# Order of work on ScalarE and VectorE in a hybrid decoder layer: late weight splits, scalings, keys and norm sums

## The chip, the cores and the metric

The kernel runs on one core of one Trainium2 chip. A core has five engines with instruction queues of their own: TensorE (PE in the profile; PEld is its weight load), VectorE (DVE), ScalarE (ACT), GpSimd (POOL) and SyncE (SP), which here only issues DMAs. The metric is the device time of one execution in microseconds (us). The kernel before has a median of 1187.84 us over three runs, from 1185.57 to 1188.33.

## The reference

One decoder layer for 512 tokens of width 1024, in float32. The normalised input goes through one combined projection that feeds two mixers. Both are merged by sigmoid gates, projected, normalised and added to the stream; a gated MLP with a short causal convolution follows.

```python
h = rms_norm(x, norm_mix_pre); z = h @ w_in
z_rwkv, z_nsa, z_gate = split(z)
o_a = rwkv7_time_mix(z_rwkv, ...)   # 16 heads of 64: state recurrence over time,
                                    # then group norm of y, bonus (r*k*r_k summed)*v, times g = sigmoid(gd) @ g2
o_b = nsa_attention(z_nsa, ...)     # compressed, selected and window branches
g_a, g_b = split(sigmoid(z_gate))
m = g_a * (o_a @ w_branch_rwkv) + g_b * (o_b @ w_branch_nsa)
x = x + rms_norm(m @ w_out, norm_mix_post)
h = rms_norm(x, norm_ffn_pre)
u = causal_dwconv(h @ ffn_up)
u_gate, u_val = split(u)
x = x + rms_norm((silu(u_gate) * u_val) @ ffn_down, norm_ffn_post)
```

## The kernel before

**Number format.** A matrix product is made of three matmuls: both operands are split into a high part (rounded by ScalarE, tile names in h) and a low part (the remainder, names in l), and high x high, high x low and low x high are summed. A weight therefore passes through `split_to` (L156): a DMA on SP's queue into a raw buffer, a copy on ScalarE (L124 in the trace), a subtraction on GpSimd or VectorE (L160). The raw buffers are a ring of WB = 3 (tag "raw"): a fourth load waits until the subtraction of the first has read its buffer. SP's queue issues in order, so what stands behind a waiting load waits too.

**Stages.** The recurrence has eight pairs of heads, p = 0 to 7, in two groups of GP = 4 pairs, g = 0 and 1. For each pair `prep` (from L506) makes decay, keys and bonus factor F, then `couple` (from L573) makes the products g<-AR,KB within chunks of 64 tokens (L597), masks them into GS (L600), transposes the scaled keys into BKT (L620), and computes LV (L626) and the bonus bv (L631). `invert` inverts the small triangular blocks of all pairs of a group on VectorE (XP, L652 and L654, the copy at L666). `recur` walks through eight chunks: xw and xs are products with the inverse (L796), UV is their copy (L800 on VectorE, L801 on ScalarE), and xs with BKT (L806) carries the state. `finish` (from L821) scales the group's output YT by the group norm's factor (L831), transposes it (gt), adds the bonus, and multiplies by pg, the product of gate activations with the weights g2 (L861 to L864). While the second group is inverted and recurred, TensorE projects gates, v, the keys of the selected and window branches (ksp and kwp; `khl`, split into kst at L950 and L951) and the queries q. Then follow eight stages of attention scores and values, the branch projections (`branch`, ub, L1181 to L1183), the output projection (wo), the second norm with its transposes (n2p), and the MLP (pu, dn).

**What sets the order.** `drive` (L439) takes steps alternately from a chain of projections (the fill) and from streams that run beside it, each at its own rate, so the program text is written in an interleaved order. A scheduler then orders the instructions of each engine; it may move an instruction ahead of its place in the program. One that is marked `tc.keep_in_program_order` keeps its place in program order. PSUM banks come in named pairs (pj, px, py, pz); a name's third use waits for the readers of its first.

**Names the prediction uses.** g20r to g27r are the raw g2 weights and gh, gl their halves; lw5r and lw6r, with lh and ll, the small weights for decay and rate of pairs 5 and 6; pw, pa, pn and pb the four PSUM tiles in `prep` (decay, rate, norm sums, broadcast norm); T the decay after tanh; rbh and rbl the halves of F.

Of the kernel before, what the change touches and what calls it, by code (L numbers as in the profile page):

```python
# [12 lines left out]
AF = mybir.ActivationFunctionType  # L13
# [19 lines left out]
GP = 4  # L33
# [9 lines left out]
def hybrid_layer(ctx: ExitStack, tc: tile.TileContext, a, out, dbg=None, stop=None):  # L43
# [109 lines left out]
    eps6 = vec[:, V_EPS:V_EPS + 1]  # L153
    epsg = vec[:, V_EPS + 1:V_EPS + 2]

    def split_to(src, hi, lo, name, n, eng=None, p=None):  # L156
        raw = (p or wp).tile([128, n], F32, tag="raw", name=name + "r", bufs=WB)
        sy.dma_start(raw, src)
        act(hi, raw, AF.Copy)
        (eng or po).tensor_tensor(lo, raw, hi.bitcast(F32), op=OP.subtract)  # L160

    def split_w(src, name):
# [346 lines left out]
    def prep(p, o, gr=None):  # L509
# [17 lines left out]
        F = rw.tile([128, S], F32, tag="T", name=f"F{p}", bufs=NT)  # L527
        sc.activation(F, pa, AF.Identity, scale=hka[:, p:p + 1], bias=oka[:, p:p + 1])
        yield
        pn = pz(f"pn{p}")  # L530
        for t in range(4):
            te.matmul(pn[:, 2 * t:2 * t + 2], Q[:, t * 128:(t + 1) * 128], sel, start=True, stop=True)
        nt = rw.tile([128, 8], F32, tag="nt", name=f"nt{p}", bufs=2)
# [27 lines left out]
        ve.tensor_tensor(KB[:, :, 0, :], pb.rearrange(c8, t=64), A.rearrange(c8, t=64), op=OP.mult)  # L561
        o.Q = None if gr else Q
        ve.scalar_tensor_tensor(gr.AR[p % GP][:, 0, :] if gr else Q, Q, -2.0, pb, op0=OP.mult, op1=OP.mult)
        ve.scalar_tensor_tensor(F, R, vec[:, V_RK + p:V_RK + p + 1], F, op0=OP.mult, op1=OP.mult)
        rbh = o.rbh = rw.tile([128, S], F32R, tag="T", name=f"rbh{p}", bufs=NT)
        sc.activation(rbh, F, AF.Copy)
        rbl = o.rbl = rw.tile([128, S], F32R, tag="T", name=f"rbl{p}", bufs=NT)
# [253 lines left out]
    def finish(gr, g):  # L821
        st = gr.st
        yield
        ve.tensor_reduce(st[:, 1, 3], gr.sq[3], axis=AX.X, op=OP.add)
        sc.activation(st[:, 0], st[:, 1], AF.Sqrt, scale=1.0 / 64, bias=epsg)
        ve.reciprocal(st[:, 1], st[:, 0])
        yield
        for i in range(GP):
            p = GP * g + i
            Y8 = gr.YT[:, :, i]  # L830
            scaled = (po if g else ve).tensor_tensor(Y8, Y8, st[:, 1, :, 2 * i:2 * i + 2, None]  # L831
                                                     .to_broadcast([128, 4, 2, 64]), op=OP.mult)
            if g == 0:
                tc.keep_in_program_order(scaled)
            gh = rh_.tile([128, 256], F32R, tag="gh", name=f"gh{p}", bufs=1)
            gl = rh_.tile([128, 256], F32R, tag="gl", name=f"gl{p}", bufs=1)
            split_to(a["g2"][p], gh, gl, f"g2{p}", 256)
            po.tensor_copy(gh[64:96, 128:], gl[64:96, 128:].bitcast(F32))
            bvl = rh_.tile([128, S], F32, tag="bvl", name=f"bvl{p}", bufs=1)
            sy.dma_start(bvl, bvd[p])  # L840
            yield
            yield
            yield
            pt = px(f"gt{p}")
            for t in range(4):
                tr(pt[:, t * 128:(t + 1) * 128], Y8[:, t].rearrange("p h v -> p (h v)"), ident)
            y2 = rh_.tile([128, S], F32, tag="TB", name=f"y2{p}", bufs=1)
            y2v = y2.rearrange("p (t s u) -> p t s u", s=2, u=64)
            ptv = pt.rearrange("p (t s u) -> p t s u", s=2, u=64)
            lnw, lnb = vec[:, V_LNW + p:V_LNW + p + 1], vec[:, V_LNB + p:V_LNB + p + 1]  # L850
            if i % 2 == 0:
                sc.activation(y2, pt, AF.Identity, scale=lnw, bias=lnb)
            else:
                for x in range(2):
                    sc.activation(y2v[:, :, x], ptv[:, :, 1 - x], AF.Identity, scale=lnw, bias=lnb)
            (ve if g else po).tensor_tensor(y2, y2, bvl, op=OP.add)
            yield
            if g:
                yield
            pg = px(f"pg{p}")  # L860
            te.matmul(pg, gh[:, :128], lg1h, start=True, stop=False)  # L861
            te.matmul(pg, gh[:, :128], lg1l, start=False, stop=False)
            te.matmul(pg, gl[:, :128], lg1h, start=False, stop=False)
            te.matmul(pg, gh[:96, 128:], lg2, start=False, stop=True)  # L864
            ve.tensor_tensor(y2, y2, pg, op=OP.mult)
            sy.dma_start(oad[p], y2)
            yield
# [97 lines left out]
    def qproj(p8):  # L965
        return split_out(27 + p8, f"q{p8}", qd[p8], 0.125)

    fr1 = [plain_out(43 + i, f"v{i}", vd_[i], zp) for i in range(1, 4)]
    fr1 += [khl(39 + i, "ssww"[i], 0, False) for i in (0, 2)]
    drive(itertools.chain(*gates_(16 - 6 - NG0, zp), *fr1, *[qproj(i) for i in range(2)], *[x for i in range(2, NQ1)  # L970
                                        for x in ((qproj(i), queries(i - 2)) if i < 4 else (qproj(i),))]),
          f0, *rt1)
    rax.close()
# [198 lines left out]
    def branch(x, o8, sh, sl):  # L1172
# [1 line left out]
        sy.dma_start(g, gtd[o8, x])  # L1174
        wh, wl = split_w(a["wb"][x, o8], f"wb{x}{o8}")
        wh, wl = wslice(wh), wslice(wl)
        if x + o8 == 0:
            yield
        p = pj(f"ub{x}{o8}")
        for k in range(KT):  # L1180
# [82 lines left out]
    with pool("bp", "left") as bp:  # L1263
# [3 lines left out]
        for _ in fill:  # L1267
            next(load, None)
        run(load)
        for o8 in range(8):  # L1270
            run(branch(1, o8, spb[0], spb[1]))
            for i in (2 * o8, 2 * o8 + 1):
                if i < NW:
                    wo_load(i, bp)
# [122 lines left out]
    for t in range(4):  # L1397
        wo_tok(t, (px, py, pj, px)[t])
        if t < NU:
            first(t)  # L1400
        if t:
            norm_t(xn[t - 1], t - 1, h2h, h2l, "n2")
        xn[t] = norm_x(x2[:, t, :], t, [g2b[:, 0:512], g2b[:, 512:]], "n2", op)
    pu4 = [py("pu0"), py("pu1"), pj("pu2")]
    for b in range(NU - 1):
        half_up(b, 0)
    norm_t(xn[3], 3, h2h, h2l, "n2")
    half_up(NU - 1, 0)
# [151 lines left out]
```

## Time and profile before

| what | value |
|---|---|
| median of three runs | 1187.84 us (1185.57 to 1188.33) |
| the profiled execution's own time | 1192.53 us |
| its span, first to last instruction | 1190.7 us |
| mean granted TensorE clock | 0.988 |
| busy: TensorE, VectorE, ScalarE, GpSimd | 1158.1, 583.6, 582.3, 583.2 us |
| instructions: TensorE, VectorE, ScalarE, GpSimd | 7414, 1208, 1149, 525 |
| HBM read and written | 108.30 and 19.14 MB |

In the profile a row of the timeline has the start in us, the duration in us, engine, line, operation, out<-in, shape and count, and in brackets how long the engine had been idle before it and what ended that. A row of the waits has the waiting engine and line, what it waited for, the sum of its waits in us, their number and the longest. Lines are those of the kernel before.

### The profile page before, as it was taken

How to read it: one execution, taken by the hardware profiler on the slowest of the kernel's cores; microseconds unless marked ns; L12 is line 12 of the kernel's file. 1: busy time of each engine (PE TensorE's matmuls, PEld its weight loads, DVE VectorE, ACT ScalarE, POOL GpSimd, SP SyncE). 2: the span in 40 equal slices, each digit the busy share in tenths (PEclk: the TensorE clock that was granted, in tenths of full speed). 3: DMA queues.
4: the chain of work that ended last, by engine and by line, in shares of the span. 5: the costliest groups of instructions: out<-in, count | busy, mean ns of one | idle time of the engine just before them, and what ended most of it. 6: DMA issues, size and time to landing. Idle time of an engine off the chain costs nothing.

```text
span 1190.7 us, 19894 instructions
## 1 busy us (share of the span) xinstructions
PE 1158.1 (97%) x7414; PEld 927.2 (78%) x7414; DVE 583.6 (49%) x1208; ACT 582.3 (49%) x1149; POOL 583.2 (49%) x525
## 2 busy tenths in 40 slices
PE   7999999999999999999999999999999999999997
PEld 6888878876778777766767777788888888888886
DVE  4225655633556561488797775654333433331103
ACT  5536653543655434277776555443444444443311
POOL 4336664434566443366567653521456655654440
PEclk8999999998999999999999999999999999999999
DMA  6522235321342654234442225551133233334421
GB/s 221 132 81 74 87 102 164 107 81 46 87 140 82 179 156 155 65 114 135 132 143 78 65 72 187 183 182 45 53 97 98 97 98 98 98 96 134 132 63 71
DMA packets 95652, 131.95 MB, mean 111 GB/s; under 512 B 34178, under 2 KB 37058, under 8 KB 95299
## 3 DMA queue, kind: packets, MB, share of 16 engines
q1 hardware_dynamic: 79634, 116.26, 31.4%
q10 hardware_dynamic: 15920, 14.42, 3.9%
q8 instruction: 58, 0.95, 0.3%
q14 instruction: 40, 0.32, 0.1%
HBM read 108.30 MB, written 19.14 MB: 107 GB/s over the span
## 4 chain that ended last, share of the span: by engine, by line
PE 60%; DVE 5%; issue 3%; ACT 2%; POOL 2%; DMA 0%; DVEq 0%; ACTq 0%; POOLq 0%
PE pu L221 6%; PE pu L219 6%; PE pu L220 6%; PE o L1124 3%; PE dn L1293 3%; PE dn L1292 3%; PE dn L1291 3%; PE pt L140 3%; PE ub L1181 2%; PE s L1068 2%; PE ub L1183 2%; PE ub L1182 2%; PE q L297 1%; PE wo L1363 1%; PE wo L1365 1%
## 5 line engine op out<-in xcount | busy, mean ns | idle before, releaser
L1077 ACT ACTIVATE p<-p,stt 128x384 f32<-128x384 f32 (+3 forms) x128 | 70.8, 554 | 41.5 <-DVE stt L1075 39.8
L1431 DVE SCALAR_TENSOR_TENSOR u<-pu,cvec,u 128x511 f32<-128x511 f32 x44 | 33.0, 749 | 102.0 <-ACT u L1430 102.0
L1051 POOL TENSOR_SCALAR p<-p,stt 128x512 f32<-128x512 f32 (+3 forms) x60 | 68.6, 1153 | 27.7 <-DVE stt L1046 21.3
L1075 DVE CUSTOM_DVE_ANT_0 p<-s,rh 128x384 f32<-128x384 f32 (+3 forms) x128 | 59.4, 484 | 26.5 <-PE s L1061 19.0
L1435 POOL TENSOR_TENSOR u<-u,u 128x512 f32<-128x512 f32 x22 | 28.4, 1290 | 38.6 <-DVE u L1432 37.7
L1437 DVE TENSOR_TENSOR al<-u,ah 128x512 fp32r<-128x512 f32 x22 | 23.9, 1085 | 45.8 <-ACT ah L1436 45.8
L140 PE MATMUL pt<-ident,p 128*128 128x128 f32 x320 | 44.8, 273 | 0.8 <-POOL p L1051 0.7
L1124 PE MATMUL o<-PT,vt 128*64 128x256 f32 (+3 forms) x256 | 45.3, 444 | 0.0
L140 PEld LDWEIGHTS pt<-ident,p 128*128 128x128 f32 x320 | 37.9, 141 | 5.7 <-POOL p L1051 1.0
L1068 PE MATMUL s<-kst,qs 128*128 128x512 f32 (+1 forms) x128 | 38.5, 392 | 3.5 <-DVE stt L1075 3.5
L1430 ACT ACTIVATE u<-pu,cvec 128x512 f32<-128x512 f32 x44 | 33.6, 764 | 5.7 <-PE pu L1395 5.7
L1051 DVE TENSOR_SCALAR p<-p,stt 128x512 f32<-128x512 f32 (+3 forms) x68 | 34.0, 531 | 0.6
L1432 DVE SCALAR_TENSOR_TENSOR u<-pu,cvec,u 128x510 f32<-128x510 f32 x44 | 32.9, 749 | 1.6
L1124 PEld LDWEIGHTS o<-PT,vt 128*64 128x64 f32 x256 | 17.5, 136 | 18.8 <-issue 16.7
L1068 PEld LDWEIGHTS s<-kst,qs 128*128 128x128 f32 x128 | 21.2, 188 | 13.0 <-DVE stt L1075 8.4
L1115 ACT ACTIVATE PT<-pt 128x512 f32<-128x512 f32 x48 | 27.3, 584 | 5.4 <-PE pt L140 5.3
L1339 DVE TENSOR_TENSOR p2tm<-dn,gb 128x512 f32<-128x512 f32 x4 | 2.8, 692 | 51.2 <-ACT p2jl L1337 51.2
L1117 DVE COPY PT<-pt 128x512 f32<-128x512 f32 x32 | 21.8, 682 | 8.4 <-PE pt L140 8.3
L1436 ACT ACTIVATE ah<-u 128x512 fp32r<-128x512 f32 x22 | 13.9, 633 | 22.4 <-POOL u L1435 22.4
L1077 ACT ACTIVATION_READ_ACCUMULATOR p<-p,stt 128x1 f32 x128 | 24.1, 188 | 0.0
L801 ACT ACTIVATE UV<-xs 64x256 f32<-64x256 f32 x16 | 6.0, 378 | 34.7 <-PE xs L796 34.1
L654 DVE TENSOR_TENSOR XP<-XP,TM 128x30 f32<-128x30 f32 (+14 forms) x60 | 20.3, 338 | 2.0
(1758 smaller groups left out, 3960.4 us busy)
## 6 DMA issues: line engine op xcount, KB each, us to landing
gtd<-gt ACTq DMA_DIRECT2D x16, 256.0 KB, 2.2
qs<-qd SPq DMA_DIRECT2D x32, 128.0 KB, 2.9
g<-gtd SPq DMA_DIRECT2D x16, 256.0 KB, 3.1
xt<-in_x_dram SPq DMA_DIRECT2D x4, 512.0 KB, 5.7
bvd<-bv SPq DMA_DIRECT2D x8, 256.0 KB, 2.4
bvl<-bvd SPq DMA_DIRECT2D x8, 256.0 KB, 2.7
oad<-y SPq DMA_DIRECT2D x8, 256.0 KB, 2.9
kst<-kst ACTq DMA_DIRECT2D x16, 128.0 KB, 2.8
```

The lines of the kernel that those rows point to most:

```text
L140: return te.transpose(o, i, ident)
L219: te.matmul(p, wh(k), mh(k), start=first and k == 0, stop=False)
L220: te.matmul(p, wh(k), ml(k), start=False, stop=False)
L221: te.matmul(p, wl(k), mh(k), start=False, stop=last and k == n - 1)
L1051: (po if b and (p8 or e) else ve).tensor_scalar(o.pe[e, b, k], o.pe[e, b, k], st[e][:, 3, i:i + 1], None, op0=OP.mult)
L1068: m = te.matmul(s_[:, :n], qt, kt[:, x, b, :n], start=x == 0, stop=x == 1)
L1075: ve.tensor_tensor_reduce(sb, parts[b], rh[e][:, (3 - qb) * 128:], -1.0, BIG, OP.add, OP.min, st[e][:, 0, i:i + 1])
L1077: sc.activation(sb, sb, AF.Exp, scale=-1.0, bias=st[e][:, 0, i:i + 1], accum_out=st[e][:, 1, i:i + 1])
L1124: te.matmul(acc[e * 64:e * 64 + 64, j * 128:], vt[:, j, b * 256 + g * 64:b * 256 + g * 64 + 64], m[e][:, c:c + n], start=False, stop=k == ...
L1291: te.matmul(acc[half, t], sh[:, k, tsl], wh[kk], start=k == 0, stop=False)
L1292: te.matmul(acc[half, t], sh[:, k, tsl], wl[kk], start=False, stop=False)
L1293: te.matmul(acc[half, t], sl[:, k, tsl], wh[kk], start=False, stop=k == n - 1)
```

## The change

Seven edits, none of which alters a value that is computed.

A. `split_to` takes `late`; the copies of the g2 weights in `finish` are marked to keep their place on ScalarE.
B. The norm sums pn take a bank of the pair px instead of pz, except in pair 4.
C. YT's scalings in `finish` are issued two pairs ahead; in group 0 the first two may be moved freely, the third and fourth keep their place.
D. Beside the second group, the keys ksp and kwp and the query q0 are projected ahead of v1 to v3, and not behind them.
E. The bonus factor's multiplication F<-R keeps its place behind AR.
F. The first half of block 0 of the up projection is issued ahead of the transposes of the second norm's third row block.
G. In the second branch's projections, a branch issues its weight loads when the branch before is halfway.

```diff
--- before.py
+++ after.py
@@ -153,10 +153,12 @@
     eps6 = vec[:, V_EPS:V_EPS + 1]
     epsg = vec[:, V_EPS + 1:V_EPS + 2]
 
-    def split_to(src, hi, lo, name, n, eng=None, p=None):
+    def split_to(src, hi, lo, name, n, eng=None, p=None, late=False):
         raw = (p or wp).tile([128, n], F32, tag="raw", name=name + "r", bufs=WB)
         sy.dma_start(raw, src)
-        act(hi, raw, AF.Copy)
+        i = act(hi, raw, AF.Copy)
+        if late:
+            tc.keep_in_program_order(i)
         (eng or po).tensor_tensor(lo, raw, hi.bitcast(F32), op=OP.subtract)
 
     def split_w(src, name):
@@ -527,7 +529,7 @@
         F = rw.tile([128, S], F32, tag="T", name=f"F{p}", bufs=NT)
         sc.activation(F, pa, AF.Identity, scale=hka[:, p:p + 1], bias=oka[:, p:p + 1])
         yield
-        pn = pz(f"pn{p}")
+        pn = (pz if p == GP else px)(f"pn{p}")
         for t in range(4):
             te.matmul(pn[:, 2 * t:2 * t + 2], Q[:, t * 128:(t + 1) * 128], sel, start=True, stop=True)
         nt = rw.tile([128, 8], F32, tag="nt", name=f"nt{p}", bufs=2)
@@ -561,7 +563,8 @@
         ve.tensor_tensor(KB[:, :, 0, :], pb.rearrange(c8, t=64), A.rearrange(c8, t=64), op=OP.mult)
         o.Q = None if gr else Q
         ve.scalar_tensor_tensor(gr.AR[p % GP][:, 0, :] if gr else Q, Q, -2.0, pb, op0=OP.mult, op1=OP.mult)
-        ve.scalar_tensor_tensor(F, R, vec[:, V_RK + p:V_RK + p + 1], F, op0=OP.mult, op1=OP.mult)
+        tc.keep_in_program_order(ve.scalar_tensor_tensor(F, R, vec[:, V_RK + p:V_RK + p + 1], F, op0=OP.mult,
+                                                         op1=OP.mult))
         rbh = o.rbh = rw.tile([128, S], F32R, tag="T", name=f"rbh{p}", bufs=NT)
         sc.activation(rbh, F, AF.Copy)
         rbl = o.rbl = rw.tile([128, S], F32R, tag="T", name=f"rbl{p}", bufs=NT)
@@ -825,16 +828,23 @@
         sc.activation(st[:, 0], st[:, 1], AF.Sqrt, scale=1.0 / 64, bias=epsg)
         ve.reciprocal(st[:, 1], st[:, 0])
         yield
+        def scaled(i):
+            Y8 = gr.YT[:, :, i]
+            m = (po if g else ve).tensor_tensor(Y8, Y8, st[:, 1, :, 2 * i:2 * i + 2, None]
+                                                .to_broadcast([128, 4, 2, 64]), op=OP.mult)
+            if g == 0 and i > 1:
+                tc.keep_in_program_order(m)
+            return Y8
+
+        ahead = [scaled(i) for i in range(2)]
         for i in range(GP):
             p = GP * g + i
-            Y8 = gr.YT[:, :, i]
-            scaled = (po if g else ve).tensor_tensor(Y8, Y8, st[:, 1, :, 2 * i:2 * i + 2, None]
-                                                     .to_broadcast([128, 4, 2, 64]), op=OP.mult)
-            if g == 0:
-                tc.keep_in_program_order(scaled)
+            Y8 = ahead[i]
+            if i + 2 < GP:
+                ahead.append(scaled(i + 2))
             gh = rh_.tile([128, 256], F32R, tag="gh", name=f"gh{p}", bufs=1)
             gl = rh_.tile([128, 256], F32R, tag="gl", name=f"gl{p}", bufs=1)
-            split_to(a["g2"][p], gh, gl, f"g2{p}", 256)
+            split_to(a["g2"][p], gh, gl, f"g2{p}", 256, late=True)
             po.tensor_copy(gh[64:96, 128:], gl[64:96, 128:].bitcast(F32))
             bvl = rh_.tile([128, S], F32, tag="bvl", name=f"bvl{p}", bufs=1)
             sy.dma_start(bvl, bvd[p])
@@ -965,9 +975,9 @@
     def qproj(p8):
         return split_out(27 + p8, f"q{p8}", qd[p8], 0.125)
 
-    fr1 = [plain_out(43 + i, f"v{i}", vd_[i], zp) for i in range(1, 4)]
-    fr1 += [khl(39 + i, "ssww"[i], 0, False) for i in (0, 2)]
-    drive(itertools.chain(*gates_(16 - 6 - NG0, zp), *fr1, *[qproj(i) for i in range(2)], *[x for i in range(2, NQ1)
+    fr1 = [khl(39 + i, "ssww"[i], 0, False) for i in (0, 2)] + [qproj(0)]
+    fr1 += [plain_out(43 + i, f"v{i}", vd_[i], zp) for i in range(1, 4)]
+    drive(itertools.chain(*gates_(16 - 6 - NG0, zp), *fr1, qproj(1), *[x for i in range(2, NQ1)
                                         for x in ((qproj(i), queries(i - 2)) if i < 4 else (qproj(i),))]),
           f0, *rt1)
     rax.close()
@@ -1174,7 +1184,7 @@
         sy.dma_start(g, gtd[o8, x])
         wh, wl = split_w(a["wb"][x, o8], f"wb{x}{o8}")
         wh, wl = wslice(wh), wslice(wl)
-        if x + o8 == 0:
+        if x or o8 == 0:
             yield
         p = pj(f"ub{x}{o8}")
         for k in range(KT):
@@ -1267,8 +1277,14 @@
         for _ in fill:
             next(load, None)
         run(load)
+        second = [branch(1, o8, spb[0], spb[1]) for o8 in range(8)]
+        next(second[0])
         for o8 in range(8):
-            run(branch(1, o8, spb[0], spb[1]))
+            for _ in range(4):
+                next(second[o8])
+            if o8 < 7:
+                next(second[o8 + 1])
+            run(second[o8])
             for i in (2 * o8, 2 * o8 + 1):
                 if i < NW:
                     wo_load(i, bp)
@@ -1398,11 +1414,13 @@
         wo_tok(t, (px, py, pj, px)[t])
         if t < NU:
             first(t)
-        if t:
+        if 0 < t < 3:
             norm_t(xn[t - 1], t - 1, h2h, h2l, "n2")
         xn[t] = norm_x(x2[:, t, :], t, [g2b[:, 0:512], g2b[:, 512:]], "n2", op)
     pu4 = [py("pu0"), py("pu1"), pj("pu2")]
-    for b in range(NU - 1):
+    half_up(0, 0)
+    norm_t(xn[2], 2, h2h, h2l, "n2")
+    for b in range(1, NU - 1):
         half_up(b, 0)
     norm_t(xn[3], 3, h2h, h2l, "n2")
     half_up(NU - 1, 0)
```

Where the scheduler puts things is not in the diff, so three places follow, word for word, as lists of one engine's instructions in order. Line numbers of the changed kernel are two to eighteen higher.

The first is ScalarE in the middle of `recur` of the first group. UV is the copy of the products xs, SQ and YT belong to the group norm, gh<-g20r is the copy of the first g2 weight. Before:

```order
L124 ACTIVATE k5h_3086<-k51r 128x512
L756 ACTIVATE YT_2606<-y_2633 128x4x64
L756 ACTIVATE YT_2606<-y_2634 128x4x64
L124 ACTIVATE gh_3231<-g20r 128x256
L801 ACTIVATE UV_866<-xs_2840 64x4x64
L801 ACTIVATE UV_866<-xs_2899 64x4x64
L767 ACTIVATE SQ_2921<-YT_2606 128x512
L471 ACTIVATE v0z<-v_2704 128x512
```

Now:

```order
L124 ACTIVATE k5h_3086<-k51r 128x512
L759 ACTIVATE YT_2606<-y_2633 128x4x64
L759 ACTIVATE YT_2606<-y_2634 128x4x64
L804 ACTIVATE UV_866<-xs_2840 64x4x64
L804 ACTIVATE UV_866<-xs_2899 64x4x64
L770 ACTIVATE SQ_2921<-YT_2606 128x512
L473 ACTIVATE v0z<-v_2704 128x512
...
L623 ACTIVATE BKT_3068<-pt_3188 128x512
L623 ACTIVATE BKT_3068<-pt_3189 128x512
L629 ACTIVATE LV_3073<-pl_3200 128x512
L124 ACTIVATE gh_3233<-g20r 128x256
L516 ACTIVATE Q_3342<-K_3078,vec 128x512
```

The copy gh<-g20r stood ahead of two UV; now it stands behind LV of pair 4, more than twenty instructions later.

The second is VectorE at the end of the second group's `invert` (TM and XP are the steps of the inversion, kst the low halves of the keys, XL the copy behind the loop). Before:

```order
L652 TENSOR_TENSOR TM_4171<-XL_4170,XP_4199 128x30
L654 TENSOR_TENSOR XP_4199<-XP_4199,TM_4171 128x30
L951 TENSOR_TENSOR kst_4159<-ksp_4446,kst_4159 64x512
L951 TENSOR_TENSOR kst_4160<-ksp_4446,kst_4160 64x512
L666 COPY XL_4170<-XP_4199 128x1024
L669 STREAM_TRANSPOSE x_4400<-XL_4170 128x1024
L670 STREAM_TRANSPOSE XL_4170<-XL_4170 128x1024
L951 TENSOR_TENSOR kst_4159<-kwp_4491,kst_4159 64x512
L675 COPY TT_3074<-XL_4170 32x32x32 x2
L951 TENSOR_TENSOR kst_4160<-kwp_4491,kst_4160 64x512
```

Now:

```order
L961 TENSOR_TENSOR kst_4160<-ksp_4323,kst_4160 64x512
L655 TENSOR_TENSOR TM_4171<-XL_4170,XP_4199 128x238
L657 TENSOR_TENSOR XP_4199<-XP_4199,TM_4171 128x14x17
L655 TENSOR_TENSOR TM_4171<-XL_4170,XP_4199 128x234
L657 TENSOR_TENSOR XP_4199<-XP_4199,TM_4171 128x13x18
L655 TENSOR_TENSOR TM_4171<-XL_4170,XP_4199 128x228
L961 TENSOR_TENSOR kst_4159<-kwp_4368,kst_4159 64x512
L657 TENSOR_TENSOR XP_4199<-XP_4199,TM_4171 128x12x19
L655 TENSOR_TENSOR TM_4171<-XL_4170,XP_4199 128x220
L657 TENSOR_TENSOR XP_4199<-XP_4199,TM_4171 128x11x20
L655 TENSOR_TENSOR TM_4171<-XL_4170,XP_4199 128x210
L961 TENSOR_TENSOR kst_4160<-kwp_4368,kst_4160 64x512
```

The four kst stood behind the loop, two of them behind the copy XL; now they stand between its steps.

The third is VectorE in `prep` and `couple` of pair 3. Before:

```order
L553 SCALAR_TENSOR_TENSOR A_1705<-K_1386,vec,A_1705 128x512
L564 SCALAR_TENSOR_TENSOR F_1673<-R_1477,vec,F_1673 128x512
L561 TENSOR_TENSOR KB_1704<-pb_1713,A_1705 128x8x64
L563 SCALAR_TENSOR_TENSOR AR_860<-Q_1659,pb_1713 128x512
L568 TENSOR_TENSOR rbl_1723<-F_1673,rbh_1721 128x512
L600 TENSOR_TENSOR GS_861<-g_1776,mask 128x4x2x64
```

Now:

```order
L555 SCALAR_TENSOR_TENSOR A_1705<-K_1386,vec,A_1705 128x512
L563 TENSOR_TENSOR KB_1704<-pb_1713,A_1705 128x8x64
L565 SCALAR_TENSOR_TENSOR AR_860<-Q_1659,pb_1713 128x512
L566 SCALAR_TENSOR_TENSOR F_1673<-R_1477,vec,F_1673 128x512
L571 TENSOR_TENSOR rbl_1723<-F_1673,rbh_1721 128x512
L603 TENSOR_TENSOR GS_861<-g_1776,mask 128x4x2x64
```

F<-R stood ahead of KB<-pb and AR; now it stands behind both. In pair 7 it is the same.

## The prediction

> **What bounds the kernel now.** I read the page's busy times first, then the waits of TensorE, the granted clock in windows around the longest, and the timeline at each.
>
> ```profile
> PE 1158.1 (97%) x7414; PEld 927.2 (78%) x7414; DVE 583.6 (49%) x1208; ACT 582.3 (49%) x1149; POOL 583.2 (49%) x525
> ```
>
> ```profile
> PE g L597 <- DVE AR L563: 2.8, 2, 1.4
> PE xs L806 <- ACT UV L801: 2.8, 1, 2.8
> PE q L297 <- DVE kst L951: 2.0, 1, 2.0
> PE gt L140 <- DVE YT L831: 1.9, 1, 1.9
> ...
> PE pn L532 <- ACT T L520: 1.4, 1, 1.4
> PE n2p L140 <- DVE n2xn L196: 1.3, 1, 1.3
> ...
> PE ub L1183 <- POOL wb13l L160: 0.6, 1, 0.6
> ...
> PE ub L1183 <- POOL wb14l L160: 0.2, 1, 0.2
> ```
>
> TensorE is busy 1158.1 of the span's 1190.7 us, so it sets the end, and only its 32.6 us of idle time and what its clock loses can be won. The view of waits names the waiting line, what it waited for, the sum in us, how often, and the longest. The edits meet eight of these rows: 2.8 + 2.8 + 2.0 + 1.9 + 1.4 + 1.3 + 0.6 + 0.2 = 13.0 us. The matmuls themselves stay; the change moves work on the other engines ahead of them. The second price of a wait stands in the windows (us of the window, busy time and count of each engine, granted clock):
>
> ```profile
> core 0: us, PE busy (x) PEld busy (x) DVE busy (x) ACT busy (x) POOL busy (x), PEclk, DMA share, GB/s
> 272.18:275.59 3.41, 1.11 (x11) 0.56 (x7) 0.43 (x2) 0.26 (x1) 0.00 (x1) 1.00 0.16 43
> 275.59:282.42 6.83, 6.35 (x84) 4.91 (x84) 1.61 (x4) 0.43 (x2) 2.45 (x4) 0.50 0.12 38
> 316.55:319.97 3.42, 2.01 (x14) 1.50 (x13) 0.69 (x1) 3.38 (x4) 1.90 (x2) 1.00 0.47 174
> 319.97:323.38 3.41, 3.41 (x12) 2.83 (x10) 2.01 (x5) 3.37 (x6) 0.71 (x2) 0.50 0.02 7
> ...
> 337.03:340.45 3.42, 3.42 (x9) 2.63 (x8) 0.63 (x2) 1.74 (x4) 2.96 (x4) 0.50 0.52 115
> ...
> 446.26:449.67 3.41, 3.41 (x9) 2.64 (x10) 0.69 (x1) 1.12 (x2) 1.27 (x1) 0.50 0.58 192
> 169.74:173.15 3.41, 1.99 (x21) 1.59 (x21) 3.35 (x4) 1.80 (x4) 2.69 (x2) 1.00 0.48 154
> 173.15:176.56 3.41, 3.41 (x35) 2.94 (x34) 2.49 (x4) 0.75 (x3) 2.17 (x3) 1.00 0.43 154
> ```
>
> Behind four of the waits (xs, pn, gt, q) the clock is granted at 0.50: once for 6.83 us with 6.35 busy, three times for 3.41. Work at half clock takes twice its time, so the windows cost 6.35 / 2 = 3.2 and three times 3.41 / 2 = 1.7, together 8.3 us. Behind the wait of g (1.4 us, TensorE busy 1.99 of 3.41 with 21 matmuls) it stayed at 1.00; behind that of pn (1.4 us, 2.01 busy, 14 matmuls) it did not. So I charge half clock only where the trace shows it.
>
> **The change part by part.**
>
> **A, late splits** (the g2 weights). The stretch on ScalarE, and the same weights' neighbours later:
>
> ```profile
> L158 SPq DMA_DIRECT2D g20r<-in_g_dram x1: 327/327/327, 271.6 to 271.6; - x1
> ...
> 275.33 0.42 ACT L124 ACTIVATE gh<-g20r 128x256 fp32r<-128x256 f32 x1 [4.54 <-DMA g20r<-in_g_dram]
> 275.66 0.36 ACT L801 ACTIVATE UV<-xs 64x256 f32<-64x256 f32 x1
> ...
> 275.83 0.72 POOL L160 TENSOR_TENSOR gl<-g20r,gh 128x256 fp32r<-128x256 f32 x1 [3.65 <-ACT gh L124]
> ...
> 302.24 0.46 SPq L158 DMA_DIRECT2D lw5r<-in_lwa_dram  x1
> ...
> 302.84 0.60 ACT L626 ACTIVATE LV<-pl 128x512 f32<-128x512 f32 x1 [0.44 <-PE pl L624]
> ...
> 305.68 0.42 ACT L124 ACTIVATE lh<-lw5r 128x256 fp32r<-128x256 f32 x1 [1.10 <-DMA lw5r<-in_lwa_dram]
> ```
>
> The copy of g20r stood ahead of UV<-xs and held ScalarE 4.54 us until its DMA, issued only at 271.6, had landed; xs L806 waited 2.8 for the UV behind it. In the new order the copy comes after LV, UV is next in line, and its 0.36 us lies beside the matmuls of v, as in the other steps of the loop (without them 0.36 would be left of the 2.8). Removed: 2.8 + 3.2 = 6.0 us. Price: g20r's raw buffer, one of three, is held until the copy at LV's end, 302.84 + 0.60 = 303.4, then 0.42 and 0.72 more: free at 304.6. In the new order the DMA of lw5r takes this buffer: 304.6 instead of 302.24, 2.4 later, and with it lh at 305.68 and, behind it on SP's queue, the loads of k6 and r6 for the next pair, for whose projections TensorE waits. That is charged in the next part.
>
> **B, norm sums in the other bank.** pn5 no longer waits until ScalarE's T has read pw5. The wait (1.4) and its window (1.7) go, 3.1. But the scaled keys further on come from the chain of ScalarE and VectorE, which this does not shorten:
>
> ```profile
> 315.91 0.63 ACT L124 ACTIVATE r6h<-r60r 128x512 fp32r<-128x512 f32 x1 [1.44 <-DMA r60r<-in_wf_dram]
> ...
> 317.85 0.69 ACT L520 ACTIVATE T<-pw,vd 128x512 f32<-128x512 f32 x1
> ...
> 328.41 0.67 DVE L563 SCALAR_TENSOR_TENSOR AR<-Q,pb 128x512 f32<-128x512 f32 x1
> ...
> 330.98 2.06 PE L597 MATMUL g<-AR,KB 64*128 64x128 f32 x32
> ```
>
> AR ends at 329.08, g starts at 330.98: 1.9 us of slack. Of the 3.1 at most 1.9 stay; the rest comes back as a wait at g. If lw5r's 2.4 reach T over r60r, whose DMA stands behind it on the queue, nothing stays. Bounds 0 and 1.9; I take 1.0.
>
> **C, YT's scalings ahead.** On VectorE the pinned scaling stood behind rbl:
>
> ```profile
> 332.93 1.35 DVE L568 TENSOR_TENSOR rbl<-F,rbh 128x512 fp32r<-128x512 f32 x1
> 334.20 1.53 DVE L831 TENSOR_TENSOR YT<-YT,gst 128x512 f32<-128x512 f32 x1
> ```
>
> It ended at 335.73, and gt waited 1.9 for it; now this scaling runs some 30 us earlier, right behind the first two. Removed: the wait and its window, 1.9 + 1.7 = 3.6. The 1.53 on VectorE are paid earlier, ahead of K<-k, where no wait of TensorE stands in the view. What is late next are the GS behind it, which also gain 1.53. Bounds 1.5 and 3.6; I take 3.0.
>
> **D, keys first.** VectorE stood idle beside group two's inversion:
>
> ```profile
> 425.31 0.20 DVE L654 TENSOR_TENSOR XP<-XP,TM 128x30 f32<-128x30 f32 x1
> 434.29 0.68 DVE L951 TENSOR_TENSOR kst<-ksp,kst 64x512 fp32r<-64x512 f32 x1 [8.78 <-ACT kst L950]
> ...
> 445.33 0.69 DVE L951 TENSOR_TENSOR kst<-kwp,kst 64x512 fp32r<-64x512 f32 x1
> ```
>
> The inversion's loop ended at 425.51, VectorE waited 8.78 for the first kst, and the last kst ended at 446.02, which q1 needed for its bank: 2.0. Now the keys are projected ahead of v1 to v3, and their four evictions and q0's, 5 x 0.7 = 3.5 us, lie inside the loop. The 8.78 idle us behind it hold these 3.5 and up to 5.3 of waiting for the first key; beyond that the copy of XP, and the inversion's end with it, would come later than now. Their DMAs on ScalarE's queue pass those of v1 to v3, which are read back only for the values, a stage later. Removed: 2.0 + 1.7 = 3.7; lower bound 2.0, if the window stays cold for another reason. I take 3.7.
>
> **E, bonus factor behind AR.** In pair 3 (and alike in pair 7):
>
> ```profile
> 169.52 1.77 DVE L564 SCALAR_TENSOR_TENSOR F<-R,vec,F 128x512 f32<-128x512 f32 x1
> 171.21 0.68 DVE L561 TENSOR_TENSOR KB<-pb,A 128x512 f32<-128x512 f32 x1
> 171.81 0.67 DVE L563 SCALAR_TENSOR_TENSOR AR<-Q,pb 128x512 f32<-128x512 f32 x1
> ```
>
> F needs 1.77 and stood ahead of KB and AR; g waits for AR, 1.4 each time. KB and AR now come 1.7 sooner, more than the wait. F, rbh and rbl follow, and with them GS: it could start 0.3 us later than now, though TensorE arrives 1.4 earlier; the pl that reads it has other work ahead of it (without that, 0.3 + 1.4 = 1.7 would be lost again at each). Bounds 1.4 and 2.8; I take 2.8.
>
> **F, half of block 0 ahead of the norm's transposes.** n2p waited 1.3 for
>
> ```profile
> 827.86 1.42 DVE L196 SCALAR_TENSOR_TENSOR n2xn<-x,n2r,gb 128x512 f32<-128x512 f32 x2
> ```
>
> It is the last row's norm, whose transposes keep their place among the matmuls; its squares may begin a little sooner. Bounds 0 and 1.3; I take 0.3. **G, the branches' loads ahead**, removes the two waits of ub, 0.6 + 0.2: 0.8, and 0 if the loads of the output weights, now behind them on SP's queue, come late.
>
> Sum: 6.0 + 1.0 + 3.0 + 3.7 + 2.8 + 0.3 + 0.8 = 17.6 us. Upper ends: 6.0 + 1.9 + 3.6 + 3.7 + 2.8 + 1.3 + 0.8 = 20.1. Lower ends, with A's clock kept cold: 2.8 + 0 + 1.5 + 2.0 + 1.4 = 7.7.
>
> The profiled execution took 1192.53: 1192.53 - 17.6 = 1174.9. The plain runs' median is 4.7 below it. If those runs have the same waits, they come to 1187.84 - 17.6 = 1170.2; if the 4.7 are cold windows that they lack (4.7 / 1.7 = 2.8 windows), the gain is 12.9 and they come to 1174.9. I take the middle, 1172.
>
> **The rivals.**
>
> *Cold windows stay.* The sparse matmuls around these places, not the waits, starve the window, so the half clock comes back. Then only waits are saved: 2.8 + 1.0 + 1.5 + 2.0 + 2.8 + 0.3 + 0.8 = 11.2, or 1176.6. For it: 1.4 us cooled at pn and not at g. Against it: all four cold windows stand right behind a wait. Chance 0.10. [...]
>
> *The chain of ScalarE takes over.* lw5r's 2.4 are not absorbed: B gives nothing, and pair 5 or 6 gets a wait of 2.4 with a window of 1.7, 4.1 us. 17.6 - 1.0 - 4.1 = 12.5; if YT's gain goes into the same chain, 9.5: 1187.84 - 9.5 = 1178.3. For it: ScalarE and GpSimd are busy 3.38 and 1.90 of the 3.42 us around 318. Against it: ScalarE waited 1.44 there for r60r's DMA, which A's 6.0 do not delay. Chance 0.15.
>
> *No change.* The ring of three raw buffers, held longer by six of the eight g2 splits (gh0 to gh2 and gh4 to gh6 move back on ScalarE), gives back the gain: each held slot that SP's queue runs into costs the same 4.1. Four of them: 17.6 - 16.4 = 1.2, 1186.6. Chance 0.08.
>
> *Slower.* The same mechanism with all six: 17.6 - 24.6 = -7.0, 1194.8; it decides from the sixth (five leave -2.9, within the noise). In group two it would sit at the loads of q7 and the next keys:
>
> ```profile
> 501.93 0.33 SPq L158 DMA_DIRECT2D q71r<-in_wf_dram  x1
> ...
> 532.03 0.61 ACT L124 ACTIVATE q7h<-q71r 128x512 fp32r<-128x512 f32 x1
> ```
>
> 30 us lie between issue and use, so a slot that is lost there should cost nothing. Chance 0.05, and 0.01 for other losses.
>
> **How the numbers follow.** The forecast has 0.61: with the first two rivals 0.86 for faster by over 0.3% (3.6 us, about what a measurement of this kernel can tell from no change), 0.08 same, 0.06 slower. The range begins at the upper ends, 1187.84 - 20.1 = 1167.7, less 4 for order that moves elsewhere (score stages of group two): 1164. It ends at the lower ends with one new wait, 7.7 - 4.1 = 3.6: 1184.
>
> **What would show it.** Right: the rows xs, pn, gt, q and both g gone from the waits, clock 1.00 around 276, 320, 337 and 446, TensorE's idle time down to about 22 us. A: ScalarE's gap of 4.54 ahead of gh gone. B: a new wait at g5 or pb5 of 1 to 2 us. Keys: no 8.78 of idle VectorE. Wrong: new waits of TensorE on lh, r6h or q7h with half clock behind them (the ring), or half clock at the same places without waits (the clock).

## The result and the profile after

The changed kernel takes 1177.55 us (median; 1176.95 to 1179.83 over four runs), the kernel before beside it 1187.59. The ratio is 0.9922, 95% interval 0.9903 to 0.9940: 9 to 10 us faster. A repetition on another chip gave 1178.16 against 1186.54, again 0.9922 (0.9904 to 0.9939). The forecast was 1172 with a range of 1164 to 1184: the direction and the range hold, the gain is about 60% of the forecast one.

The page of the changed kernel has these rows for TensorE's busy time and its granted clock in 40 slices of the span:

```profile
PE 1153.3 (98%) x7414; PEld 923.4 (78%) x7414; DVE 580.7 (49%) x1208; ACT 579.6 (49%) x1149; POOL 581.4 (49%) x525
...
PEclk8999999999999999989999999999999999999999
```

The span went from 1190.7 to 1176.3 us, TensorE's idle time from 32.6 to 23.0. One slice after the start, near 520 us, shows a lowered clock. The waits of TensorE:

```profile
PE r L301 <- POOL r6l L162: 1.5, 1, 1.5
PE pg L871 <- ACT nt L536: 1.2, 1, 1.2
PE n2p L140 <- DVE n2xn L198: 1.2, 1, 1.2
...
PE pt L140 <- ACT p L1087: 0.7, 1, 0.7
PE ub L1193 <- POOL wb13l L162: 0.7, 1, 0.7
...
PE s L1071 <- DVE y L875: 0.4, 1, 0.4
...
PE g L600 <- DVE AR L565: 0.2, 1, 0.2
```

The rows xs, pn, gt and q are gone, and g is down from 2.8 to 0.2. At pair 5 one row is new (pg on nt) and one has grown from 0.3 (r on r6l); two are new in the first score stage (pt on p L1087, s on y); n2p and ub stand as before. How far TensorE is ahead at each place, from the start of the same matmul in both timelines (us from the span's start; the first row is taken off, since it starts at 33.97 to 36.25 in the fourteen profiles). The letters say which edit acts on that stretch; a difference also holds whatever chance the two profiled executions had there:

| matmul | before | after | ahead | gained since the row above |
|---|---|---|---|---|
| first of kc | 35.15 | 34.24 | 0 | |
| g, pair 2 | 146.67 | 145.14 | 0.6 | 0.6 (E, pairs 0 to 2) |
| g, pair 3 | 172.54 | 169.48 | 2.2 | 1.5 (E) |
| g, pair 4 | 294.47 | 286.76 | 6.8 | 4.6 (A) |
| g, pair 5 | 330.98 | 322.83 | 7.2 | 0.4 (B) |
| g, pair 6 | 362.62 | 351.20 | 10.5 | 3.3 (C) |
| g, pair 7 | 388.49 | 375.55 | 12.0 | 1.5 (E) |
| first of vtp (behind the second recurrence) | 510.93 | 493.86 | 16.2 | 4.1 (D) |
| last of kwp, second half | 593.26 | 579.24 | 13.1 | -3.0 |
| first of wo | 775.45 | 760.99 | 13.5 | 0.4 (G) |
| last matmul | 1183.73 | 1169.01 | 13.8 | 0.3 (F) |

The places answer to the prediction's rows one by one. Timeline of the changed kernel, ScalarE, SP, VectorE:

```profile
274.15 0.38 ACT L804 ACTIVATE UV<-xs 64x256 f32<-64x256 f32 x1 [4.14 <-PE xs L799]
...
295.62 0.41 ACT L124 ACTIVATE gh<-g20r 128x256 fp32r<-128x256 f32 x1
...
296.88 0.35 SPq L158 DMA_DIRECT2D lw5r<-in_lwa_dram  x1
...
168.75 0.68 DVE L565 SCALAR_TENSOR_TENSOR AR<-Q,pb 128x512 f32<-128x512 f32 x1
169.34 1.62 DVE L566 SCALAR_TENSOR_TENSOR F<-R,vec,F 128x512 f32<-128x512 f32 x1
...
404.93 0.68 DVE L961 TENSOR_TENSOR kst<-ksp,kst 64x512 fp32r<-64x512 f32 x1 [4.09 <-ACT kst L960]
...
420.77 1.22 DVE L669 COPY XL<-XP 128x1024 f32<-128x1024 f32 x1
```

UV now waits for its product alone; gh<-g20r comes behind LV. AR ends at 169.43, when g starts (169.48), and F follows. VectorE waits 4.09 for the first key inside the loop, and the copy XL starts 45.2 us behind the g of pair 7, where it stood 48.5 behind it.

The profiled executions are 14.4 us apart, the medians 10.0. The profiled execution of before (1192.53) lies 4.9 above its median, that of the change (1178.10) 0.6 above: 14.4 - 4.9 + 0.6 = 10.1.

### The profile page after: what moved, and what is told of

Read it like the earlier page. It is cut to its first block, busy times and chain, and to the rows that moved or that the text cites. A ratio compares the mean times of both kernels' runs of the same rounds, so it can differ in the third digit from the quotient of the medians.

```text
span 1176.3 us, 19883 instructions
## 1 busy us (share of the span) xinstructions
PE 1153.3 (98%) x7414; PEld 923.4 (78%) x7414; DVE 580.7 (49%) x1208; ACT 579.6 (49%) x1149; POOL 581.4 (49%) x525
## 4 chain that ended last, share of the span: by engine, by line
PE 86%; DVE 5%; issue 3%; ACT 2%; POOL 2%; DMA 1%; SPq 0%; DVEq 0%; POOLq 0%; ACTq 0%
PE pu L222 6%; PE pu L221 6%; PE pu L223 6%; PE o L1134 4%; PE dn L1307 3%; PE dn L1308 3%; PE dn L1309 3%; PE pt L140 3%; PE gt L299 2%; PE gt L301 2%; PE gt L300 2%; PE ub L1191 2%; PE v L300 2%; PE v L299 2%; PE s L1078 2%
## 5 line engine op out<-in xcount | busy, mean ns | idle before, releaser
L1087 ACT ACTIVATE p<-p,stt 128x384 f32<-128x384 f32 (+3 forms) x128 | 70.7, 554 | 40.7 <-DVE stt L1085 39.3
L1087 ACT ACTIVATION_READ_ACCUMULATOR p<-p,stt 128x1 f32 x128 | 24.1, 188 | 0.0
```

What stands on the lines that cost most here:

```text
L1087: sc.activation(sb, sb, AF.Exp, scale=-1.0, bias=st[e][:, 0, i:i + 1], accum_out=st[e][:, 1, i:i + 1])
```

## The experiments

Each kernel below ran with the kernel before beside it on the same chip. Two theories stood against each other. The first: the profiled execution of before overstates what its waits cost in plain runs, and the change loses something of its own in the first score stage. The second: every part is worth its wait and its cold window, and what was lost is chance.

### The loss behind 495 us

Between vtp and the second half of the keys 3.0 us are given back, and a window there has half clock:

```profile
517.50:524.33 6.83, 6.30 (x22) 3.53 (x21) 4.78 (x15) 1.56 (x4) 4.83 (x7) 0.50 0.32 100
```

Late splits in group 0 alone:

```diff
-            split_to(a["g2"][p], gh, gl, f"g2{p}", 256, late=True)
+            split_to(a["g2"][p], gh, gl, f"g2{p}", 256, late=g == 0)
```

> The g2 splits keep their place on ScalarE only in group 0; group 1's go back to the scheduler. Between the last wait of the second recurrence and the end of the first score stages the profiled execution of the changed kernel is 3.0 us slower than before (17.1 us ahead at 495, 14.0 at 587). Theory 'late pins of group two reorder the first score stage': this comes back, 1174.5 us, and the new waits of pt on p L1087 and of s on y L875 are gone. Rival 'a chance cold window of 6.8 us at 517': plain runs stay at 1177.5 +- 1, whatever the profile shows.

Measured: 1176.02 us, 0.9895 of before (0.9879 to 0.9911). The profile is 16.2 us ahead at the last of kwp instead of 13.1, and the rows of pt on ACT p and s on DVE y are gone. To set it against the change on one chip, both ran again.

> The changed kernel once more, as the measure for the three beside it: 0.992 of before, 9 to 10 us.

> The changed kernel with late splits in group 0 alone, once more on the chip of the changed kernel. Theory 'the pins of group two cost 3.1 us between the second recurrence and the second half of the keys': 3 us faster than the changed kernel. Rival 'a cold window of 6.8 us by chance in its profile': equal to it within 1 us.

Measured: the change 1178.16 (0.9922, 0.9904 to 0.9939), with late splits in group 0 alone 1175.57 (0.9900, 0.9881 to 0.9920). The six runs of the one lie between 1177.43 and 1179.01, the six of the other between 1174.56 and 1176.79; they don't overlap. So the pins of group two cost 2.6 us in plain runs, and this is no chance of one profile. The profile of the repeated change has half clock there for 3.41 us instead of 6.83 and is 14.8 ahead at the last of kwp, where the first was 13.1: the other 3.41 us cost 1.7. What is left is order and the remaining window. What the pins move shows on SP and ScalarE, first in the repeated change, then with late splits in group 0 alone:

```profile
498.63 0.33 SPq L158 DMA_DIRECT2D q71r<-in_wf_dram  x1
...
504.85 0.40 ACT L124 ACTIVATE gh<-g24r 128x256 fp32r<-128x256 f32 x1
```

```profile
486.24 0.33 SPq L158 DMA_DIRECT2D q71r<-in_wf_dram  x1
...
457.42 0.42 ACT L124 ACTIVATE gh<-g24r 128x256 fp32r<-128x256 f32 x1 [1.96 <-DMA g24r<-in_g_dram]
```

g24r's copy comes 47 us later, its raw buffer is held as long, and q71r is issued 12 us later. TensorE's order moves with it: the second half of ksp begins at 529.5 instead of 543.4, so projections that fill the first score stage are used up sooner. Which of these makes the waits of pt and s was not separated; that the pins of group two do it was. In the profile of A alone, where the keys still stand behind v1 to v3, 0.8 us are given back on this stretch, without half clock.

### Edit A undone, and alone

```diff
-            split_to(a["g2"][p], gh, gl, f"g2{p}", 256, late=True)
+            split_to(a["g2"][p], gh, gl, f"g2{p}", 256)
```

> The changed kernel with edit A undone in both groups. By the profiled pair A is worth 4.7 us at 276 and costs 3.0 in the first score stages if the pins of group two do that: 1177.5 + 4.7 - 3.0 = 1179.2 us. By the prediction (6.0, nothing lost): 1183.5. If plain runs have no cold window behind xs and the score stages lose nothing by the pins: 1177.5 + 2.8 = 1180.3.

Measured: 1180.24 us, 0.9926 (0.9911 to 0.9942), nearest to the third number, though one of its conditions is refuted above: the score stages do lose 2.6 by the pins. Without A the change is worth as much as with it, within the intervals (0.9926 against 0.9922); with A in group 0 alone, 0.9895 and 0.9900, it is worth three to four us more. Beside this run, on the same chip, late splits in group 0 alone took 1176.02: the pins of group 0 are worth 4.2 us within the change, and those of group two take back 2.6. At pair 4's g the profile is 4.7 ahead and that of the change 6.8: the 2.1 that xs waited in this execution.

The kernel before with A alone (the lines of `split_to` and of its call in the diff above):

> The kernel before with edit A alone. Theory 'plain runs mostly lack the cold windows that the profiled execution of before had, so an edit is worth the idle time that it removes': -2.8 for xs, and something back in the first score stages: -1 to -2.8 us. Rival 'wait and window, as predicted': -4.7 to -6.0 us.

Measured: 1185.80 us, 0.9980 (0.9971 to 0.9989), 2.4 us. The wait of xs is gone from its profile, but another has grown, from 1.4 before (1.6 to 1.8 with D, C or E alone):

```profile
PE pn L534 <- ACT T L522: 2.6, 1, 2.6
```

A part of the gain comes back there, as pn's chain on ScalarE does not come sooner by as much as TensorE does. The 2.4 us hold the loss by the pins of group two as well: its profile has the rows of pt on ACT p (0.7) and s on DVE y (0.4) too.

### The other edits alone

The kernel before with D alone:

> The kernel before with edit D alone. Idle time only: -2.0 us. Wait and window: -3.7 us. The profiled pair showed 4.1 between pairs 7 and the second recurrence, so if the third account (order behind the keys gains too) holds, -4 us in plain runs.

Measured: 1186.15 us, 0.9977 (0.9965 to 0.9988), 2.7 us: between idle time alone and wait with window.

With C alone:

> The kernel before with edit C alone. Idle time only: -1.9 us. Wait and window: -3.0 to -3.6 us. If the chain of ScalarE and GpSimd is next in line: 0 to -1.

Measured: 1187.42 us, 0.9991 (0.9981 to 1.0001), 1.1 us, not told apart from nothing. With E alone:

> The kernel before with edit E alone. Both theories: -2.8 us, as g's two waits had no cold window behind them; -1.4 or less if F, rbh, rbl and GS are late next.

Measured: 1185.89 us, 0.9982 (0.9971 to 0.9993), 2.1 us. The four alone add up to 2.4 + 2.7 + 1.1 + 2.1 = 8.3 of the 9.3 us of the change; A's 2.4 is already less the loss of group two's pins.

The four profiles also hold the waits that each edit left alone, once more. Rows of C alone, D alone, E alone, and of the change without A, in this order:

```profile
PE xs L806 <- ACT UV L801: 2.4, 1, 2.4
PE q L297 <- DVE kst L958: 2.0, 1, 2.0
PE r L299 <- POOL r6l L160: 1.9, 1, 1.9
```

```profile
PE xs L806 <- ACT UV L801: 1.2, 1, 1.2
```

```profile
PE q L297 <- DVE kst L952: 2.0, 1, 2.0
...
PE xs L807 <- ACT UV L802: 1.1, 1, 1.1
```

```profile
PE xs L809 <- ACT UV L804: 2.1, 1, 2.1
```

xs waited 2.8, 2.4, 1.2, 1.1 and 2.1 us in five executions in which the order at that place was the same: the landing of g20r decides; its copy starts 3.7, 3.3, 2.1, 2.0 and 3.0 us behind the issue of its DMA. The prediction had the largest of the five. q waited 2.0 each time, but the clock behind it differs, with C alone and with E alone (columns as in the prediction's windows):

```profile
437.46:440.88 3.42, 2.75 (x13) 1.94 (x11) 3.38 (x4) 1.12 (x2) 1.29 (x1) 1.00 0.60 147
440.88:444.29 3.41, 2.08 (x9) 1.78 (x10) 1.85 (x3) 1.12 (x2) 0.48 (x1) 1.00 0.52 160
444.29:447.70 3.41, 3.41 (x43) 2.63 (x43) 0.00 (x0) 0.63 (x1) 2.08 (x2) 1.00 0.73 248
```

```profile
435.27:438.68 3.41, 1.51 (x7) 1.28 (x8) 2.20 (x3) 1.11 (x2) 0.00 (x0) 1.00 0.50 145
438.68:442.10 3.42, 3.42 (x10) 2.55 (x8) 0.21 (x1) 0.64 (x2) 1.67 (x2) 0.50 0.69 240
```

The same wait of 2.0 us left the clock at 1.00 once and halved it once (where the two differ, stands in the last section). Over the profiles in which the waits of xs, pn, gt and q stand (before, the four edits alone, the change without A or without B), half clock followed in 2 of 5, 4 of 6, 2 of 3 and 3 of 4, and only once, in the profile of before, for 6.83 us.

What half clock costs can be read from these profiles too: the time from the end of each wait to a later matmul, in us, with full clock behind the wait and with half clock. Executions in which the wait itself or the order on the stretch differs (A alone, B undone) are left out.

| from the end of the wait of | to | full clock | half clock |
|---|---|---|---|
| xs | g, pair 4 | 16.31, 16.30, 16.32 (D, E, change without A) | 17.55 (C, for 3.41), 18.40 (before, for 6.83) |
| pn | g, pair 5 | 12.35, 12.36 (C, E) | 12.39, 12.39 (before, D) |
| gt | g, pair 6 | 24.93 (E) | 26.74, 26.68 (before, D) |
| q | first of vtp | 63.02 (C) | 64.76, 64.75 (before, E) |

So half clock cost 1.8 and 1.7 behind gt and q, as the prediction charged (behind q, in the profile of before, the 128x512 matmuls start 0.43 us apart at half clock and 0.23 at full, 1.8 times where it took twice), 2.1 behind xs for 6.83 us (1.2 for 3.41), and nothing behind pn. There the time comes back as a wait. TensorE before, then with C alone:

```profile
318.59 1.05 PE L532 MATMUL pn<-sel,Q 128*128 128x2 f32 x8 [1.41 <-ACT T L520]
...
329.67 0.50 PE L299 MATMUL r<-hh,r6l 128*128 128x512 f32 x1 [0.32 <-POOL r6l L160]
```

```profile
318.40 1.05 PE L532 MATMUL pn<-sel,Q 128*128 128x2 f32 x8 [1.77 <-ACT T L520]
...
329.45 0.50 PE L299 MATMUL r<-hh,r6l 128*128 128x512 f32 x1 [1.92 <-POOL r6l L160]
```

r6l comes from GpSimd 11 us behind pn in both; at half clock TensorE arrives 1.6 later and waits 1.6 less. The wait of r is therefore 0.3 with half clock behind pn (before, D alone) and 1.9 without (C alone, E alone). It stands ahead of gt's place, so it is not gt's wait moved on. The 1.1 of C alone (0 to 2.3 by its interval) has room for its idle time of 1.9, but not for the 3.6 of wait and half clock. Why it isn't more stays open; 0.9 of its profile's lead goes between the last of kwp and wo, where ub waits for weights 1.8 instead of 0.8.

### Edit B and the chain of pair 5

```diff
-        pn = (pz if p == GP else px)(f"pn{p}")
+        pn = pz(f"pn{p}")
```

> The changed kernel with pn back in the pair pz (edit B undone). Theory 'B is worth little, since its wait only moves to pg and r6l' (0.4 us by the profiled pair): the wait of pn on T comes back with 1.4, those of pg on nt and r on r6l go, 1178 us. Rival 'B is worth the wait and a cold window': 1180.5 us.

Measured: 1179.13 us, 0.9920 (0.9904 to 0.9936), against 0.9922 with B. B is worth nothing that these runs can tell. In the profile without it pn waits 2.1 on T, not the 1.4 expected, with half clock behind it; the waits of pg on nt and of r on r6l are gone, and g of pair 5 is 0.5 us behind that of the change. The changed kernel's TensorE and GpSimd show why:

```profile
313.68 0.50 PE L871 MATMUL pg<-lg1h,gh 128*128 128x512 f32 x1 [1.23 <-ACT nt L536]
321.52 0.51 PE L301 MATMUL r<-hh,r6l 128*128 128x512 f32 x1 [1.52 <-POOL r6l L162]
```

```profile
316.32 1.76 POOL L582 TENSOR_TENSOR AR<-R,EC 128x512 f32<-128x512 f32 x1 [1.58 <-ACT EC L548]
318.04 1.75 POOL L866 TENSOR_TENSOR y<-y,bvl 128x512 f32<-128x512 f32 x1
319.74 1.72 POOL L162 TENSOR_TENSOR r6l<-r61r,r6h 128x512 fp32r<-128x512 f32 x1
```

pn runs without a wait, but the next matmul in the same pair of banks, pg, waits for nt<-pn, ScalarE's reading of pn, which stands behind a table load of 1.28 us; and r6l stands on GpSimd behind AR, which waits for EC, and y. The pair py in place of px, on top of late splits in group 0 alone:

```diff
-        pn = (pz if p == GP else px)(f"pn{p}")
+        pn = (pz if p == GP else py)(f"pn{p}")
```

> As the last, but the norm sums pn take a bank of the pair py instead of px, so that pg of pair 1's finish no longer stands behind nt. Theory 'the chain of ScalarE and GpSimd sets the pace at r6l': the wait of pg on nt (1.2) goes, that of r on r6l (1.5) grows by as much, time equal within 0.5 us. Rival 'the bank made the wait': 1.2 us faster.

Measured: 1176.05 us, 0.9903 (0.9884 to 0.9921), against 1175.57: equal. The wait moved once more, by the same 1.2 us, to the broadcast norm:

```profile
PE pb L140 <- POOL nte L544: 1.2, 1, 1.2
```

So the chain sets the pace there and no bank does. r6l's wait stayed at 1.5 and did not grow as expected, since pb stands ahead of it and takes the 1.2.

The slot held by g20r was tried with a raw buffer of their own for the small weights, first in all pairs, on the changed kernel:

```diff
-        raw = (p or wp).tile([128, n], F32, tag="raw", name=name + "r", bufs=WB)
+        raw = (p or wp).tile([128, n], F32, tag="rawl" if own else "raw", name=name + "r", bufs=1 if own else WB)
...
-        split_to(a["lwa"][p], o.lh, o.ll, f"lw{p}", 256)
+        split_to(a["lwa"][p], o.lh, o.ll, f"lw{p}", 256, p=rw, own=True)
```

> The changed kernel, but the small weights lw (decay and rate) get a raw buffer of their own, so lw5r and lw6r no longer wait for a ring slot that g20r or g22r holds. Theory 'the held slot sets the pace of pair 5' (lw5r was issued 2.4 us later against BKT than before): T comes 0.8 us sooner, the waits of pg on nt (1.2) and of r on r6l (1.5) shrink by 1 to 1.5 in sum, 1176.3 us. Rival 'three table loads on ScalarE and the line of AR, y and r6l on GpSimd set it': waits as they are, 1177.5 +- 0.7.

Measured: 1186.53 us, 0.9984 (0.9969 to 0.9998), a miss of 10 us: nearly the whole gain is lost, at places that neither theory spoke of (the last section). Then for pairs 5 to 7 alone, with late splits in group 0 alone:

```diff
+        split_to(a["lwa"][p], o.lh, o.ll, f"lw{p}", 256, p=rw if p > GP else None, own=p > GP)
```

> As the second, but the small weights of pairs 5 to 7 have a raw buffer of their own, pairs 0 to 4 as they were. Theory 'the slot held by g20r delays lw5r and with it pair 5': T and EC come 0.8 us sooner, pg on nt and r on r6l shrink, 0.8 to 1.5 us faster. Rival 'not on the path': equal within 0.5 us. If the saved time comes back at pair 6, as between the fifth and sixth g of the earlier kernel with a buffer of its own: equal, with the profile ahead at g of pair 5 and level at pair 6.

Measured: 1177.46 us, 0.9916 (0.9897 to 0.9935), against 1175.57 without: not faster, rather slower. Its profile is 1.1 us further ahead at pair 5's g (8.3 against 7.2) and 0.3 behind at pair 6's (10.2 against 10.5). The gain is real at pair 5 and comes back at pair 6 as

```profile
PE g L600 <- DVE AR L565: 2.0, 1, 2.0
```

The held slot is therefore on the path of pair 5, as the prediction had it, and worth nothing in the sum of this kernel; the last section has more rows of this kind.

The fastest version is the change with late splits in group 0 alone: 1175.57 and 1176.02 us in two sets, 0.9900 and 0.9895 of before.

## Why the prediction was right, and where its sum failed

The time lies in the range and the direction is right, because the waits that it named fell. The terms, against the profiled pair and against plain runs of one edit alone:

| term | forecast | profiled pair | alone, plain runs |
|---|---|---|---|
| A | 6.0 | 4.6, and part of the -3.0 behind 495 | 2.4; group 0's pins within the change 4.2 |
| B | 1.0 | 0.4 | 0 (left out: 0.9920 against 0.9922) |
| C | 3.0 | 3.3 | 1.1 |
| D | 3.7 | 4.1 | 2.7 |
| E | 2.8 | 3.7 | 2.1 |
| F | 0.3 | 0.3 | not run |
| G | 0.8 | 0.4 | not run |
| score stage | 0 | -3.0 | -2.6 (group two's pins) |

**The step that failed first: half clock charged as if it followed each of these waits every time.** 8.3 us of half clock were read from one profiled execution and entered the terms A to D. In it all four stretches of half clock came together, 17.1 us between the first projections and the last matmul (start and end hold 10.6 more). Over the profiles with these waits it followed in 11 of 18 cases, and where it did it cost 1.8 and 1.7 at gt and q, but 2.1 and not 3.2 at xs, and nothing at pn. The plain runs agree: in 63 of the kernel before, on three chips, the mean clock was 0.989 to 0.998, 0.9945 in the mean. Taking all that is below 1.00 as half clock, a run has 2 x 0.0055 x 1187 = 13 us of it; the start and end of the fourteen profiles hold 7.9 in the mean, which leaves some 5 where the profile of before has 17.1. The prediction saw the 4.7 between profile and median and named cold windows as one reading of it, but went halfway; taken whole, its own figure of 1174.9 would have been nearer.

An estimate from these profiles: with xs's mean wait of 1.9 and each window's price by its share, A is 1.9 + 0.7 = 2.6, C 1.9 + 1.2 = 3.1, D 2.0 + 1.3 = 3.3, E 3.7 by the profiled pair; B nothing. That is 12.7, less 2.6 for the score stage 10.1, where 8.4 and 10.0 were measured. It leaves out F and G, rests on three to five profiles for each wait, and does not account for C, D and E alone, which gave less.

**The step that was missing: the pins in group two.** The prediction weighed the held raw buffer there as a rival for a slower kernel, and set it at nothing because 30 us lie between q71r's load and use. The loads did come 12 us later without a wait on them; the loss came with the order of the first score stage. It is 2.6 us, and the sum had 0 for it.

**A was over-sized twice.** The wait of xs was the longest of five executions (2.8, mean 1.9), and its window cost 2.1 and not 3.2. That small matmuls waiting for each other in the recurrence lose less from half clock was not tested. The 4.6 of the profiled pair has the same luck in it, the longest wait and the only window of 6.83. What the pins of group 0 gave within the change, 4.2, is still two thirds of the 6.0.

**B: the mechanism right, the place wrong.** The chain of ScalarE and GpSimd gave back the gain, but at pg (nt) and at r6l and not at g. lw5r's delay came as worked out: issued 3.3 us behind BKT's start (296.88 against 293.60) where it had been 0.9 behind it (302.24 against 301.31), 2.4 later.

**C, D and E** stand within 1 us of the profiled pair, in which half clock stood behind gt and q: luck of that execution for these two terms. D's loop took the keys inside its idle time as described (4.09 of waiting of the 5.3 allowed). E gave 0.2 more in each of pairs 0 to 2, where the view of waits had no row. In plain runs alone all three gave less, C least.

**F and G.** n2p waits 1.2 as it did 1.3: its norm starts from x, which is no earlier. Of the 0.3 between wo and the last matmul that is 0.1. ub's wait on wb13l stayed at 0.7; the 0.4 between kwp and wo is put down to the loads ahead by place alone.

**The rivals.** "The chain takes over" has the nearest number, 1178.3, and is right that B gives nothing and that pair 5 gets new waits; but half clock behind these waits and the loss of C's gain did not come, and the score stage's 2.6 was not in it. "Cold windows stay" (1176.6) has another mechanism than what happened: in the profile of the change the windows behind those waits are gone, and the plain runs had few to lose. The ring as a rival for no change or slower showed its shape in group two with one price of 2.6, far from six times 4.1.

## What to carry to other kernels

One profiled execution gives a wait one value; before summing, look at the mean clock of the plain runs, and price idle time by its wait and half clock only by the share of runs that show it (here 11 of 18). A pin that helps at one place is applied wherever its helper is called: the same line in the second group cost 2.6 of the 4.2 that it won in the first, so pin by place. A wait that ends at a chain moved along it here from bank to bank (pn 1.4 us, pg 1.2, pb 1.2, with r6l's 1.5 behind); a change of bank is worth what the next wait on that chain leaves, and half clock ahead of such a wait cost nothing (12.39 us from pn to g of pair 5, against 12.36 at full clock).

## What the runs showed of the hardware that was not expected

**Changes of the granted clock lay on a grid of 3.41 us.** The same waits of 1.1 to 2.8 us were followed by half clock in 11 of 18 cases. In each of the fourteen profiles all changes of the granted clock lie whole multiples of 3.413 us apart (275.59 and 446.26 before: 50 of them), and the program starts at another place of this grid each time (the first half clock begins at 9.35 us of the span before, at 8.96 with the change). The stretches of half clock behind the waits are 3.41 or 6.83 us long, one or two steps of it. With E alone q's wait, which ends at 437.17, falls into one step of the grid and leaves TensorE 1.51 us busy in it; half clock follows. With C alone it ends at 442.21 and the boundary at 440.88 cuts it: 2.75 and 2.08 us busy, full clock. Between 30 us and the last matmul of the fourteen profiles all eleven steps with 1.0 to 1.5 us busy were followed by half clock, and three of the 19 with 1.8 to 2.0; four fuller ones (2.3 to 2.5), all in the first score stage, were too, so the busy time alone does not settle it there. No run set the phase, and what makes the clock change was not shown.

**VectorE and GpSimd reading EC at once.** With a raw buffer of their own for the small weights in all pairs, g waited for AR in six places:

```profile
PE g L600 <- DVE AR L565: 9.6, 6, 2.0
...
90.70 1.80 DVE L556 SCALAR_TENSOR_TENSOR Q<-K,vec,EC 128x512 f32<-128x512 f32 x1 [1.54 <-ACT EC L548]
...
90.75 1.21 POOL L582 TENSOR_TENSOR AR<-R,EC 128x512 f32<-128x512 f32 x1 [0.91 <-ACT EC L548]
```

In the changed kernel the same two are

```profile
90.12 0.75 DVE L556 SCALAR_TENSOR_TENSOR Q<-K,vec,EC 128x512 f32<-128x512 f32 x1 [1.54 <-ACT EC L548]
...
90.17 1.76 POOL L582 TENSOR_TENSOR AR<-R,EC 128x512 f32<-128x512 f32 x1 [0.91 <-ACT EC L548]
```

Both wait for EC and start 0.05 us apart; in one kernel VectorE's takes 0.75 and GpSimd's 1.76, in the other 1.80 and 1.21. One of the two takes 0.5 to 1.1 us longer than in the other kernel, and when it is VectorE, whose chain leads to AR and g, TensorE waits. From this Q to AR VectorE runs the same instructions in the same order in both kernels; Q, KB<-F and A<-K take 2.7 us more. In pair 4, where they do not meet, Q takes 0.75 and AR 1.18 (before); the longer times, 1.76 and 1.80, come near the sum of these, 1.93. The fourteen profiles have 98 such meetings (pair 4 has none). In six of them VectorE's Q was the longer, about 1.8: five in the kernel with the raw buffer of their own in all pairs, and the one of pair 6 in the kernel with it in pairs 5 to 7. In these six g waited 1.5 to 2.0 for AR; in the others 0.2 at most, but for the 1.4 of pairs 3 and 7 where F stands ahead of AR. So the 9.6 us, and the 2.0 at pair 6 above, go with a long Q in such a meeting each time; no run took the meeting away, and why one of the two takes longer, and which, was not shown.
